# Scaling both halves of the inner RMS norms on VectorE, and issuing the local heads' O products one scheduling step later

## The chip, the cores and the metric

The kernel runs on one core of a Trainium2 chip. The metric is the device time of one execution in microseconds, as the median of several runs. TensorE is called PE here (its weight loads PEld), VectorE DVE, ScalarE ACT, GpSimd POOL and SyncE SP. Each engine executes its own instructions in the order in which the program lists them, and waits on semaphores for the others. A DMA is issued from the queue of one engine (here SP or POOL), in that queue's order.

## The reference

A two-layer decoder trunk on x of 512 tokens by 1024 features, in float32. Layer 0 mixes tokens by three groups of dilated window attention with 8 heads each, layer 1 by a gated linear recurrence. Each mixer and each ConvFFN stands between two RMS norms.

```python
for layer in range(DEPTH):                      # DEPTH = 2
    h = rms_norm(x, norm_mix_pre[layer])
    h = dilated_attention_mixer(h, ...) if layer % 2 == 0 else rglru_mixer(h, ...)
    x = x + rms_norm(h, norm_mix_post[layer])
    h = rms_norm(x, norm_ffn_pre[layer])
    h = conv_ffn(h, ...)
    x = x + rms_norm(h, norm_ffn_post[layer])
# rms_norm(x, g) = x * rsqrt(mean(x*x, -1) + 1e-6) * g
# attention, per head and group: o = softmax(q k^T * scale + bias, masked) v
# local group: window 128, dilation 1; its o is later mixed with the two strided groups by their softmax sums
```

## The kernel before

**Tiles.** The 512 tokens are four token tiles of 128 rows (t = 0 to 3). The normalised activations stand transposed in `hT` (feature on the partition, token along the row), as a rounded high part and a remainder (`hi`, `lo`). Each fp32 product is three PE passes: high times high, high times low, low times high. Weights are loaded as `raw` by DMA (some, called `sum`, are added up in memory by POOL's DMAs), split by ACT into `whi` (L253) and by DVE into `wlo` (L265), and kept in eight slots ahead of PE.

**Order.** The program is written out by hand: a stretch of PE products is followed by `tick()`, which lets side generators go on. A side that says `yield n` goes on n ticks later. So the numbers after `yield` place the side's instructions in every engine's order; nothing is reordered at run time.

**Local heads.** `local(h, ...)` is such a side, one for each of the 8 heads. It computes the scores `S` on PE (L1307), the biased row maxima on DVE (L1268) and the exponentials on ACT (L1323), transposes blocks on DVE (L1328), writes them to memory (`ltd`, L1283) and reads them back in the transposed place (`PT`, L1292), both from SP's queue. Then it says `yield 2`, and then multiplies `PT` with the values on PE into the bank `O` (L1346, 14 matmuls), copies it out on ACT (L1348) and writes it to memory from SP (`o0d`, L1350). Heads 0 and 1 wait after that `yield` for the values to exist, so that their place is set by the values.

**Inner norms.** There are three places where one sub-layer ends and the next one starts with a norm: attention to the first FFN (near 470 to 502 us of the span), first FFN to the recurrence (832 to 875 us) and recurrence to the second FFN (994 to 1024 us). At each, `norms` runs once for each token tile: `postnorm` reads the PE banks `acc`, squares them on ACT (L443, `junk`), multiplies by the gain on DVE (L547, `post`) and adds to x (L552). `prenorm` then squares x on ACT (L443), multiplies x by the gain on DVE (L477), gets the root on ACT (L450) and refines the reciprocal root on DVE with four small operations (L451 to L454), which leave two factors `y` and `q`, each one number for a row. L480 multiplies them to one factor; then the first half of the row (512 elements, `xs[0]`) is scaled on DVE (L481) and the second half (`xs[1]`) on ACT (L482). Three or four ticks later PE transposes both halves (L490, `tr`), ACT rounds them into `hT` (L499), and DVE takes the remainder (L500).

Of the kernel before, what the change touches and what calls it, by code (L numbers as in the profile page):

```python
# [14 lines left out]
AF = mybir.ActivationFunctionType  # L15
ALU = mybir.AluOpType
# [79 lines left out]
def kernel(  # L96
# [28 lines left out]
    nc = tc.nc  # L125
# [16 lines left out]
    def gen(dt=F32, s="g"):  # L142
        return gp.tile([P, 512], dt, tag="g", name=nm(s))

    def psum(s="ps"):
        return pp.tile([P, 512], F32, tag="ps", name=nm(s))

    def small(cols, s="s"):
        return sp.tile([P, cols], F32, tag=f"s{cols}", name=nm(s))
# [288 lines left out]
    def rms(parts, before=None, after=None):  # L438

        ss, b, v, y, q = small(2), small(1), small(1), small(1), small(1)  # L440
        for i, h in enumerate(parts):
            junk = gen(s="junk")
            nc.scalar.activation(junk, h, AF.Square, accum_out=ss[:, i : i + 1])  # L443
            if i == 0:
                if before:
                    before()
                nc.vector.tensor_scalar(b, ss[:, 0:1], 1.0 / D, EPS, op0=ALU.mult, op1=ALU.add)
        if after:
            after()
        nc.scalar.activation(y, ss[:, 1:2], AF.Sqrt, scale=1.0 / D, bias=b)  # L450
        nc.vector.scalar_tensor_tensor(v, ss[:, 1:2], 1.0 / D, b, op0=ALU.mult, op1=ALU.add)  # L451
        nc.vector.reciprocal(y, y)
        nc.vector.scalar_tensor_tensor(q, y, v, y, op0=ALU.mult, op1=ALU.mult)
        nc.vector.tensor_scalar(q, q, -0.5, 1.5, op0=ALU.mult, op1=ALU.add)  # L454
        return y, q
# [10 lines left out]
    def halves(ap):  # L466
        return [ap[:, 0:512], ap[:, 512:1024]]
# [4 lines left out]
    def prenorm(t, hT, g, wait, paired=True):  # L472
        xh, gh = halves(xs_sb[t]), halves(g)
        xs = [gen(s="xs") for _ in range(2)]

        def gained(i):
            nc.vector.tensor_tensor(xs[i], xh[i], gh[i], op=ALU.mult)  # L477

        y, q = rms(xh, lambda: gained(0), lambda: gained(1))
        nc.vector.tensor_tensor(q, y, q, op=ALU.mult)  # L480
        nc.vector.tensor_scalar(xs[0], xs[0], q, None, op0=ALU.mult)  # L481
        nc.scalar.activation(xs[1], xs[1], AF.Identity, scale=q)  # L482
        yield wait
        transposed(t, xs, hT, (0, 1), paired)

    def transposed(t, xs, hT, parts=(0, 1), paired=False):
        for i in parts:
            ps = psum("tr")
            for k in range(4):
                nc.tensor.transpose(ps[:, k * P : (k + 1) * P], xs[i][:, k * P : (k + 1) * P], ident)  # L490
            ps3 = ps.rearrange("p (k c) -> p k c", k=4)
            hi, lo = (h[:, 4 * i : 4 * i + 4, t * P : (t + 1) * P] for h in hT)
            if paired:
                ps3 = ps.rearrange("p (k c a) -> p k a c", k=4, a=2)
                hi, lo = (
                    h[:, 4 * i : 4 * i + 4, :].rearrange("p k (a c) -> p k a c", a=2)[:, :, :, 64 * t : 64 * t + 64]
                    for h in hT
                )
            nc.scalar.activation(hi, ps3, AF.Copy)  # L499
            nc.vector.tensor_tensor(lo, ps3, hi.bitcast(F32), op=ALU.subtract)  # L500
# [578 lines left out]
    def attention(hT, post, pre, spill):  # L1079
# [46 lines left out]
        def toeplitz(*which):  # L1126

            ask()
            key, T = asked.pop(0)
            assert key == which  # L1130
            return T
# [132 lines left out]
        def vtile(vs, t, part):  # L1264
            return vs[t].rearrange("p (b a) -> p a b", a=2)[:, part // 2, part % 2 * P : part % 2 * P + P]

        def scores(dst, ps, bias, mx, over=3 * NEG):
            nc.vector.tensor_tensor_reduce(  # L1268
                dst, ps, bias, scale=1.0, scalar=over, op0=ALU.add, op1=ALU.max, accum_out=mx
            )  # L1270

        def strips(t):
            return t.rearrange("p (j m k) -> p j m k", j=4, m=4)

        def in_strips(ap):
            return ap.rearrange("p (j k) -> p j k", j=4)

        def by_fours(ap):
            return ap.rearrange("p (k j) -> p j k", j=4)

        def to_dram(t, ms, name):
            d = dp.tile([P, 512], F32, name=name)
            nc.sync.dma_start(strips(d)[:, :, ms, :], strips(t)[:, :, ms, :])  # L1283
            return d

        def from_dram(d, ms):

            t = gen(s="PT")
            w = 32 * (ms.stop - ms.start)
            src = bass.AP(tensor=d.tensor, offset=d.offset + 32 * ms.start, ap=[[P, P], [32 * 512, 4], [1, w]])  # L1290
            dst = t.rearrange("p (i c) -> p i c", i=4)[:, :, 32 * ms.start : 32 * ms.stop]
            nc.sync.dma_start(dst, src)  # L1292
            return t.rearrange("p (i m q) -> p m i q", i=4, m=4)

        def weights_of(L, a, j0):
            m = 2 * (a % 2)
            return L[a // 2].rearrange("p (j c) -> p j c", j=4)[:, :, 32 * (m + j0) : 32 * (m + 2)]

        def local(h, hh, q, k, v):
            T = toeplitz(0, h)  # L1300
            L = [gen(s="L") for _ in range(2)]
            Sp = [psum("S") for _ in range(2)]
            mx = small(4)
            for a in range(4):
                o = (a % 2) * 256
                lo, k0 = (P, 0) if a == 0 else (0, (a - 1) * P)
                mm(Sp[a // 2][:, o + lo : o + 256], q[hh][:, a * P : (a + 1) * P], k[hh][:, k0 : (a + 1) * P],  # L1307
                   start=True, stop=True)
            for a in range(4):
                o = (a % 2) * 256  # L1310
                lo = P if a == 0 else 0
                for j in range(lo // P, 2):
                    c = slice(o + j * P, o + j * P + P)
                    scores(
                        strips(L[a // 2])[:, :, 2 * (a % 2) + j, :], in_strips(Sp[a // 2][:, c]), by_fours(T[:, j * P : j * P + P]),
                        mx[:, a : a + 1], mx[:, a : a + 1] if j and a else 3 * NEG,
                    )
            neg = small(4)
            nc.vector.tensor_scalar(neg, mx, -1.0, None, op0=ALU.mult)
            nc.vector.tensor_copy(st0[:, :, 0, h], mx)  # L1320
            for a in range(4):
                ls = weights_of(L, a, 1 if a == 0 else 0)
                nc.scalar.activation(ls, ls, AF.Exp, bias=neg[:, a : a + 1], accum_out=st0[:, a, 1, h : h + 1])  # L1323
            yield 1
            turned = [gen(s="LT") for _ in range(2)]
            skip = slice(1, 4), slice(0, 4)
            for c in range(2):
                nc.vector.transpose(strips(turned[c])[:, :, skip[c], :], strips(L[c])[:, :, skip[c], :])  # L1328
            yield 1
            placed = [to_dram(turned[c], skip[c], f"ltd{h}{c}") for c in range(2)]  # L1330
            yield 2
            pts = {}
            for c in range(2):
                pt = from_dram(placed[c], skip[c])
                for m in range(4):
                    pts[2 * c + m // 2, m % 2] = pt[:, m]
            yield 2
            if len(v) < 4:
                while len(v) < 4:
                    yield 1  # L1340
                yield 1 + h
            po = psum("O")
            for a in range(4):
                js = [1] if a == 0 else [0, 1]
                for j in js:
                    mm(po[:, a * P : (a + 1) * P], vtile(v, a - 1 + j, h % 4), pts[a, j], start=j == js[0], stop=j == 1)  # L1346
            o = gen(s="o0")
            nc.scalar.activation(o, po, AF.Copy)  # L1348
            od = dp.tile([P, 512], F32, name=f"o0d{h}")
            nc.sync.dma_start(od, o)  # L1350
            o0[h] = od
# [163 lines left out]
        for hp in range(4):  # L1515
            q, k = [], []
# [345 lines left out]
```

## Time and profile before

| what | value |
|---|---|
| median of 3 runs | 1384.68 us (1384.51 to 1389.64) |
| the profiled execution | 1389.3 us, its span 1387.5 us |
| PE busy | 1355.5 us (98%) |
| DVE busy | 1048.3 us (76%) |
| ACT busy | 679.5 us (49%) |
| POOL busy | 111.3 us (8%) |
| mean granted PE clock | 0.996 |
| moved by DMA | 243.11 MB |

The span runs from the first to the last instruction of the profiled execution; all starts are counted from its beginning. In a row of the timeline the columns are start, duration, engine, line, operation, output<-input and count, and in brackets the time for which the engine had been idle and what released it. In a row of the windows the clock (PEclk) stands behind the busy times of the five engines, then the DMA share. In a row of the waits stand total, count and longest wait.

### The profile page before, as it was taken

The page shows a single profiled execution, that of the slowest core. Times are in us where ns is not written, and L with a number is a line of the kernel's source. Part 1 is how long each engine was busy: PE and PEld are TensorE (multiplying, and loading weights), DVE is VectorE, ACT ScalarE, POOL GpSimd, SP SyncE. Part 2 cuts the span into 40 slices and gives each one's busy share as a digit, 9 for nine tenths or more (in the row PEclk, how much of TensorE's full clock was granted, in tenths as well). Part 3 has the DMA queues.
Part 4 walks back from the last instruction along what each step waited for, and adds up shares of the span by engine and source line. Part 5 has one row for each costly group of instructions (what it writes and reads, how often), then busy time and mean ns, then how long its engine had stood idle before and what let it go on. Part 6 is the DMA issues. An engine that isn't in the chain of part 4 may idle for free.

```text
span 1387.5 us, 18700 instructions
## 1 busy us (share of the span) xinstructions
PE 1355.5 (98%) x7109; PEld 1200.3 (87%) x7109; DVE 1048.3 (76%) x1838; ACT 679.5 (49%) x1137; POOL 111.3 (8%) x126
## 2 busy tenths in 40 slices
PE   8999999999999989999999999999999999999997
PEld 6888888888888889998888888888899998888886
DVE  7786574636767678897978789778878897958785
ACT  5434342414355563455545545579663455535452
POOL 1211012011000001000000020000001000000020
PEclk9999999999999999999999999999999999999999
DMA  8979679696648264565767793233153665758771
GB/s 256 241 219 276 161 181 262 199 217 180 222 154 305 85 187 103 158 167 127 193 183 193 200 269 126 92 122 121 61 156 99 167 167 128 187 161 213 206 203 61
DMA packets 184237, 243.11 MB, mean 175 GB/s; under 512 B 16632, under 2 KB 135936, under 8 KB 184146
## 3 DMA queue, kind: packets, MB, share of 16 engines
q1 hardware_dynamic: 151456, 184.82, 40.7%
q0 software_dynamic: 32688, 57.09, 21.4%
q8 instruction: 56, 0.92, 0.3%
q14 instruction: 35, 0.29, 0.1%
q10 hardware_dynamic: 2, 0.00, 0.0%
HBM read 218.23 MB, written 28.36 MB: 178 GB/s over the span
## 4 chain that ended last, share of the span: by engine, by line
PE 30%; DVE 25%; ACT 9%; DMA 4%; issue 3%; DVEq 0%; ACTq 0%; SPq 0%; POOLq 0%
PE ps L436 16%; DVE wlo L265 7%; PE vq L634 5%; PE acc L436 5%; DVE u L822 5%; PE vq L436 3%; ACT whi L253 2%; DMA sum<-in_ffn_w_down_dram 2%; DVE xb L1581 1%; DVE x L552 1%; ACT u L818 1%; DVE run L609 1%; DVE post L547 1%; DMA raw<-in_ffn_w_up_dram 1%; DVE u L834 1%
## 5 line engine op out<-in xcount | busy, mean ns | idle before, releaser
L436 PE MATMUL ps<-hT,whi 128*128 128x512 f32 (+1 forms) x2528 | 698.8, 362 | 2.1 <-DVE hT L500 1.5
L436 PEld LDWEIGHTS ps<-hT,whi 128*128 128x128 f32 x2528 | 460.1, 190 | 59.2 <-DVE hT L500 2.2
L436 PE MATMUL ps<-hT,wlo 128*128 128x512 f32 (+1 forms) x1264 | 456.6, 361 | 1.5 <-DVE wlo L265 1.5
L265 DVE TENSOR_TENSOR wlo<-raw,whi 128x1024 fp32r<-128x1024 f32 x233 | 280.0, 1217 | 24.5 <-ACT whi L253 24.2
L253 ACT ACTIVATE whi<-raw 128x1024 fp32r<-128x1024 f32 x233 | 239.0, 1051 | 119.8 <-DMA raw<-in_attn_w_qkv_dram 82.9
L436 PEld LDWEIGHTS ps<-hT,wlo 128*128 128x128 f32 x1264 | 240.3, 190 | 29.8 <-DVE wlo L265 1.9
L822 DVE SCALAR_TENSOR_TENSOR u<-ps,cols,u 128x511 f32<-128x511 f32 (+1 forms) x160 | 119.5, 747 | 71.2 <-ACT u L818 68.3
L253 ACT ACTIVATE whi<-sum 128x1024 fp32r<-128x1024 f32 x68 | 70.7, 1050 | 143.8 <-DMA sum<-in_ffn_w_down_dram 65.2
L634 PE MATMUL vq<-whi,A 128*128 128x512 f32 x448 | 137.8, 379 | 0.0
L265 DVE TENSOR_TENSOR wlo<-sum,whi 128x1024 fp32r<-128x1024 f32 x68 | 81.9, 1217 | 57.6 <-ACT whi L253 57.6
L436 PE MATMUL acc<-whi,alo 128*128 128x512 f32 x256 | 97.2, 380 | 1.7 <-DVE alo L185 1.6
L436 PE MATMUL acc<-whi,ahi 128*128 128x512 f32 x256 | 98.2, 383 | 0.0
L436 PE MATMUL acc<-wlo,ahi 128*128 128x512 f32 x256 | 97.2, 380 | 0.6 <-DVE wlo L265 0.6
L634 PEld LDWEIGHTS vq<-whi,A 128*128 128x128 f32 x448 | 84.7, 189 | 12.0
L634 PE MATMUL vq<-wlo,A 128*128 128x512 f32 x224 | 85.1, 380 | 2.1 <-DVE wlo L265 2.1
L832 ACT ACTIVATE u<-u 128x512 f32<-128x512 f32 x48 | 30.3, 632 | 110.4 <-DVE u L822 110.4
L818 ACT ACTIVATE u<-ps,cols 128x512 f32<-128x512 f32 x80 | 61.0, 763 | 4.6 <-PE ps L436 4.6
L634 PE MATMUL vq<-whi,T 128*128 128x512 f32 x192 | 59.7, 382 | 0.0
L436 PEld LDWEIGHTS acc<-whi,alo 128*128 128x128 f32 x256 | 48.4, 189 | 9.2 <-DVE alo L185 2.5
L436 PEld LDWEIGHTS acc<-wlo,ahi 128*128 128x128 f32 x256 | 48.4, 189 | 7.8 <-DVE wlo L265 1.4
L436 PEld LDWEIGHTS acc<-whi,ahi 128*128 128x128 f32 x256 | 48.4, 189 | 6.6 <-ACT ahi L184 0.2
L634 PEld LDWEIGHTS vq<-wlo,A 128*128 128x128 f32 x224 | 42.3, 189 | 8.8 <-DVE wlo L265 2.9
(247 smaller groups left out, 1782.3 us busy)
## 6 DMA issues: line engine op xcount, KB each, us to landing
raw<-in_ffn_w_up_dram SPq DMA_DIRECT2D x44, 1024.0 KB
raw<-in_attn_w_qkv_dram SPq DMA_DIRECT2D x25, 1024.0 KB
raw<-in_ffn_w_down_dram SPq DMA_DIRECT2D x16, 1024.0 KB
sum<-in_ffn_w_down_dram POOLq DMA_DIRECT2D x16, 1024.0 KB, 8.7
sum<-in_attn_w_qkv_dram POOLq DMA_DIRECT2D x24, 512.0 KB, 8.4
raw<-in_attn_w_qkv_dram SPq DMA_DIRECT2D x16, 512.0 KB
sum<-in_ffn_w_down_dram SPq DMA_DIRECT2D x8, 1024.0 KB
raw<-in_lru_w_in_dram SPq DMA_DIRECT2D x8, 1024.0 KB
```

Of the source, the lines that this page charges most:

```text
L253: nc.scalar.activation(hi, raw, AF.Copy)
L265: nc.vector.tensor_tensor(lo, raw, hi.bitcast(F32), op=ALU.subtract)
L436: mm(dst, l[a], r[b], start=start and n == 0, stop=stop and n == 2)
L547: nc.vector.tensor_tensor(in_two(u[i]), unwoven(banks[i]), in_two(gh[i]), op=ALU.mult)
L552: nc.vector.scalar_tensor_tensor(xh[i], u[i], y, xh[i], op0=ALU.mult, op1=ALU.add)
L609: nc.vector.tensor_tensor(r[h], a, b[:, k], op=ALU.add if sg > 0 else ALU.subtract)
L634: mm(banks[u], act(a)[:, 2 * j + k, u * P : (u + 1) * P], woven(W[b][:, k, :]), start=(j, k, n) == (0, 0, 0), stop=(j, k, n) == (1, 1, 2),)
L818: nc.scalar.activation(u, ps, AF.Identity, scale=cc[:, j : j + 1], bias=cc[:, 48 + j : 49 + j])
L822: nc.vector.scalar_tensor_tensor(u[:, d:], ps[:, : S - d], wc, u[:, d:], op0=ALU.mult, op1=ALU.add)
L832: nc.scalar.activation(u, u, AF.Gelu_apprx_tanh)
L834: nc.vector.tensor_tensor(gv[k], gv[k], u, op=ALU.mult)
L1581: nc.vector.scalar_tensor_tensor(u[:, d:], ps[:, : S - d], wc, u[:, d:], op0=ALU.mult, op1=ALU.add)
```

## The change

```diff
         y, q = rms(xh, lambda: gained(0), lambda: gained(1))
-        nc.vector.tensor_tensor(q, y, q, op=ALU.mult)
-        nc.vector.tensor_scalar(xs[0], xs[0], q, None, op0=ALU.mult)
-        nc.scalar.activation(xs[1], xs[1], AF.Identity, scale=q)
+        for i in range(2):
+            nc.vector.tensor_scalar(xs[i], xs[i], y, q, op0=ALU.mult, op1=ALU.mult)
         yield wait
         transposed(t, xs, hT, (0, 1), paired)
...
                 pt = from_dram(placed[c], skip[c])
                 for m in range(4):
                     pts[2 * c + m // 2, m % 2] = pt[:, m]
-            yield 2
+            yield 3
             if len(v) < 4:
```

The first edit is executed 12 times (three places, four token tiles). DVE loses the product of two columns (L480) and gains the second half; both halves are now multiplied by two factors in one operation. ACT loses L482. All other instructions keep their order. Lines after L480 are one lower in the changed kernel.

The second edit moves the O product of heads 2 to 7, each with its ACT copy and its SP write; heads 0 and 1 keep their place. POOL's order is unchanged.

On PE, before, in the third pair of local heads. `O_1289` is head 0, `O_1301<-PT_1204` is head 2, and `S_1317` are the scores of head 4:

```order
L1346 MATMUL O_1289<-PT_924,c_363 128x128 x2
L1346 MATMUL O_1289<-PT_924,c_364 128x128
L1346 MATMUL O_1301<-PT_1204,v_365 128x128 x2
L1346 MATMUL O_1301<-PT_1204,v_366 128x128
L1346 MATMUL O_1301<-PT_1206,v_366 128x128
L1346 MATMUL O_1301<-PT_1206,c_363 128x128 x2
L1346 MATMUL O_1301<-PT_1206,c_364 128x128
L1307 MATMUL S_1317<-qk_1165,qk_1000 128x128
L1307 MATMUL S_1317<-qk_1165,qk_1000 128x256
```

Head 2's product stands directly behind head 0's, and head 4's scores behind it. The same place on PE now:

```order
L1345 MATMUL O_1289<-PT_924,c_363 128x128 x2
L1345 MATMUL O_1289<-PT_924,c_364 128x128
L1306 MATMUL S_1305<-qk_1165,qk_1000 128x128
L1306 MATMUL S_1305<-qk_1165,qk_1000 128x256
L1306 MATMUL S_1306<-qk_1165,qk_1000 128x256 x2
L436 MATMUL ps_1330<-hT_85,whi_1129 128x512
```

The scores follow head 0 at once, then a feature product of 24 matmuls into `ps_1330`. Behind that product PE now has head 1 and then head 2 (`PT_1204`):

```order
L1345 MATMUL O_1357<-PT_962,c_363 128x128 x2
L1345 MATMUL O_1357<-PT_962,c_364 128x128
L1345 MATMUL O_1369<-PT_1204,v_365 128x128 x2
L1345 MATMUL O_1369<-PT_1204,v_366 128x128
L1345 MATMUL O_1369<-PT_1206,v_366 128x128
L1345 MATMUL O_1369<-PT_1206,c_363 128x128 x2
L1345 MATMUL O_1369<-PT_1206,c_364 128x128
L1306 MATMUL S_1389<-qk_1201,qk_1056 128x128
```

So head 2 is one feature product later. Head 3 likewise goes behind two value products of 24 matmuls each.

On DVE, before, at the end of token tile 3's norm in the first place (`s_4482` is `y`, `s_4483` is `q`, `tr_4552` belongs to token tile 2, `tr_4590` to tile 3):

```order
L453 SCALAR_TENSOR_TENSOR s_4483<-s_4482,s_4481 128x1
L454 TENSOR_SCALAR s_4483<-s_4483 128x1
L480 TENSOR_TENSOR s_4483<-s_4482,s_4483 128x1
L481 TENSOR_SCALAR xs_4477<-xs_4477,s_4483 128x512
L500 TENSOR_TENSOR hT_3933<-tr_4552,hT_3932 128x8x64
L500 TENSOR_TENSOR hT_3933<-tr_4559,hT_3932 128x8x64
L500 TENSOR_TENSOR hT_3933<-tr_4590,hT_3932 128x8x64
```

And now:

```order
L453 SCALAR_TENSOR_TENSOR s_4480<-s_4479,s_4478 128x1
L454 TENSOR_SCALAR s_4480<-s_4480 128x1
L481 TENSOR_SCALAR xs_4474<-xs_4474,s_4479,s_4480 128x512
L481 TENSOR_SCALAR xs_4475<-xs_4475,s_4479,s_4480 128x512
L499 TENSOR_TENSOR hT_3933<-tr_4548,hT_3932 128x8x64
L499 TENSOR_TENSOR hT_3933<-tr_4555,hT_3932 128x8x64
L499 TENSOR_TENSOR hT_3933<-tr_4586,hT_3932 128x8x64
```

The small product is gone and the second half stands behind the first, ahead of tile 2's remainders. On ACT, before, at the same place:

```order
L450 ACTIVATE s_4482<-s_4479,s_4480 128x1
L482 ACTIVATE xs_4478<-xs_4478,s_4483 128x512
L499 ACTIVATE hT_3932<-tr_4552 128x8x64
L499 ACTIVATE hT_3932<-tr_4559 128x8x64
L499 ACTIVATE hT_3932<-tr_4590 128x8x64
```

And now:

```order
L450 ACTIVATE s_4479<-s_4476,s_4477 128x1
L498 ACTIVATE hT_3932<-tr_4548 128x8x64
L498 ACTIVATE hT_3932<-tr_4555 128x8x64
L498 ACTIVATE hT_3932<-tr_4586 128x8x64
L498 ACTIVATE hT_3932<-tr_4593 128x8x64
```

Between the root (L450) and token tile 2's evictions ACT no longer has anything that waits for DVE's factors. In the same way, after L450 of tiles 0 and 2 in the first place the next on ACT is now the squaring of the next tile's banks, and after L450 of tile 1 the next weight split (`whi`).

## Prediction

> **What bounds the kernel now.** I read the page's head first, then the waits of PE, then the timeline of PE at the longest of them, and last the timeline of DVE and ACT ahead of those.
>
> ```profile
> span 1387.5 us, 18700 instructions
> PE 1355.5 (98%) x7109; PEld 1200.3 (87%) x7109; DVE 1048.3 (76%) x1838; ACT 679.5 (49%) x1137; POOL 111.3 (8%) x126
> ...
> PE tr L490 <- DVE xs L481: 7.1, 5, 3.1
> PE O L1346 <- DMA PT<-ltd: 2.2, 1, 2.2
> ...
> PE ps L436 <- DVE wlo L265: 1.5, 1, 1.5
> ```
>
> PE is the bound: 98% busy, the rest a few waits. An edit can gain only in what PE waits for, and in PE's clock. The two longest entries are what this change touches: the transposes of the inner norms wait 7.1 us for the scaled rows, and one O product waits 2.2 us for `PT` from memory.
>
> **The O products.** PE's timeline at the third pair of heads, and the same work a little later without a wait:
>
> ```profile
> 133.29 1.68 PE L1346 MATMUL O<-PT,v 128*128 128x128 f32 x8 [2.17 <-DMA PT<-ltd]
> ...
> 136.04 2.44 PE L1307 MATMUL S<-qk,qk 128*128 128x128 f32 x8
> 138.13 0.78 PE L436 MATMUL ps<-hT,whi 128*128 128x512 f32 x2
> ...
> 143.50 1.10 PE L1346 MATMUL O<-PT,v 128*128 128x128 f32 x8
> ...
> 145.14 1.11 PE L1346 MATMUL O<-PT,v 128*128 128x128 f32 x8
> ...
> 146.79 1.68 PE L1307 MATMUL S<-qk,qk 128*128 128x128 f32 x8
> 148.12 0.57 PE L634 MATMUL vq<-whi,hT 128*128 128x512 f32 x1
> ```
>
> The head-2 product starts 2.17 us late, and is then slow itself: 136.04 - 133.29 = 2.75 us against 146.79 - 145.14 = 1.65 us for the same 14 matmuls; the scores behind it take 138.13 - 136.04 = 2.09 against 148.12 - 146.79 = 1.33 us. That is 1.1 + 0.8 = 1.9 us more. The windows say why:
>
> ```profile
> 133.30:136.00 2.70, 2.70 (x14) 2.60 (x15) 0.00 (x0) 0.00 (x0) 0.00 (x0) 0.66 1.10 341
> ...
> 501.00:503.00 2.00, 1.95 (x18) 1.95 (x19) 1.25 (x3) 2.00 (x5) 0.00 (x0) 1.00 0.90 296
> ...
> 872.50:875.00 2.50, 2.50 (x14) 2.50 (x13) 0.73 (x1) 0.42 (x1) 0.00 (x0) 0.53 0.13 52
> ```
>
> The granted clock was 0.66 behind this wait. It was also 0.53 at 872.5 to 875 us, behind a row of smaller waits in the second norm place, which cost there (1 - 0.53) x 2.5 = 1.2 us; and it stayed at 1.00 at 501 us, behind the longest wait of all (3.15 us, below). So a dip follows some waits and not others.
>
> The edit puts 1.33 us of scores and a product of 24 matmuls (5.4 us, as from 138.13 to 143.50) ahead of head 2, and head 1's product (1.65): PE reaches it near 133.29 - 2.17 + 1.33 + 5.37 + 1.65 = 139.5 us, and `PT` was there at 133.3. The wait goes whole: 2.2 us, and the 1.9 us with it. What else is moved: for heads 2 to 7, 14 matmuls with their weight loads, an ACT copy and an SP write each. PE does the same work in another order, at no cost. On ACT the copy of head 3 now waits for a product behind two value products; behind it stand weight splits that PE uses a product and more later (10 us), which is their cover; without it PE would wait about 1 us for each. On SP the write of head 3 goes behind a weight load and two value writes, so that this load no longer queues behind it; POOL's order is the same, and its table loads wait for score maxima, which come earlier with PE. The `PT` buffers are held one step longer; two later `PT` loads now wait for PE, for products over some 10 us before. Next to be late after this is the weight remainder at 359 us (1.5 us, above).
>
> The Trainium skill ("TensorE: Matmul & The Clock Gate", Part 1) says that the clock is halved after an idle window of about 3.4 us on a free-running grid. The dip here came behind 2.17 us, so the trace does not bear out that length, and by that rule the dip would not be this wait's; the sum without it is the third rival.
>
> **The norms.** First the price of a scale with two factors, which the trace does not have.
>
> ```profile
> L552 DVE SCALAR_TENSOR_TENSOR x<-post,s,x 128x512 f32<-128x512 f32 x32 | 22.6, 748 | 0.6
> L481 DVE TENSOR_SCALAR xs<-xs,s 128x512 f32<-128x512 f32 x12 | 5.8, 486 | 0.4
> L1629 DVE TENSOR_SCALAR th<-th 128x512 f32<-128x512 f32 x8 | 3.4, 426 | 0.3
> ...
> L453 DVE SCALAR_TENSOR_TENSOR s<-s,s 128x1 f32<-128x1 f32 x28 | 6.1, 219 | 1.0
> L451 DVE SCALAR_TENSOR_TENSOR s<-s,s 128x1 f32<-128x1 f32 x28 | 4.2, 150 | 0.0
> ```
>
> A column as a factor costs 60 to 69 ns over a constant (486 against 426, 219 against 150). So two factors: 486 + 60 = 546 ns, my value, as the nearest form; the low end is 486 (the second factor costs nothing), the high end 748 (the rate of the operation with two tensors).
>
> The Trainium skill ("VectorE: DVE Perf Modes", the perf-mode tier table) lets a float32 scale from SBUF run at two elements a cycle, and names no charge for factors. By it the operation stays at 486 ns and the sum below is 1.1 us lower.
>
> ```profile
> 472.07 0.16 DVE L480 TENSOR_TENSOR s<-s,s 128x1 f32<-128x1 f32 x1
> 473.59 0.69 DVE L547 TENSOR_TENSOR post<-acc,gain 128x512 f32<-128x512 f32 x1 [0.84 <-ACT junk L443]
> 479.05 0.16 DVE L480 TENSOR_TENSOR s<-s,s 128x1 f32<-128x1 f32 x1
> 480.95 1.23 DVE L265 TENSOR_TENSOR wlo<-raw,whi 128x1024 fp32r<-128x1024 f32 x1 [1.21 <-ACT whi L253]
> 493.33 0.16 DVE L480 TENSOR_TENSOR s<-s,s 128x1 f32<-128x1 f32 x1
> 494.85 0.69 DVE L547 TENSOR_TENSOR post<-acc,gain 128x512 f32<-128x512 f32 x1 [0.84 <-ACT junk L443]
> ...
> 836.59 0.16 DVE L480 TENSOR_TENSOR s<-s,s 128x1 f32<-128x1 f32 x1
> 838.49 2.36 DVE L265 TENSOR_TENSOR wlo<-raw,whi 128x1024 fp32r<-128x1024 f32 x2 [1.22 <-ACT whi L253]
> 847.74 0.16 DVE L480 TENSOR_TENSOR s<-s,s 128x1 f32<-128x1 f32 x1
> 849.17 1.29 DVE L500 TENSOR_TENSOR hT<-tr,hT 128x512 fp32r<-128x512 f32 x2 [0.75 <-ACT hT L499]
> 860.82 0.16 DVE L480 TENSOR_TENSOR s<-s,s 128x1 f32<-128x1 f32 x1
> 861.42 0.68 DVE L648 TENSOR_TENSOR c<-acc,c 128x512 f32<-128x512 f32 x1
> 868.17 0.16 DVE L480 TENSOR_TENSOR s<-s,s 128x1 f32<-128x1 f32 x1
> ...
> 1015.83 0.69 DVE L547 TENSOR_TENSOR post<-acc,gain 128x512 f32<-128x512 f32 x1 [0.84 <-ACT junk L443]
> ...
> 478.00 0.30 ACT L450 ACTIVATE s<-s,s 128x1 f32<-128x1 f32 x1
> ...
> L253 ACT ACTIVATE whi<-raw 128x1024 fp32r<-128x1024 f32 x233 | 239.0, 1051 | 119.8 <-DMA raw<-in_attn_w_qkv_dram 82.9
> ```
>
> Where nothing waits (860.82 to 861.42), L480 and L481 occupy DVE for 0.60 us, of which 0.20 is L480; so one scale takes a slot of 0.40, with two factors 0.46, and the new pair 0.92 us. Alone that is 0.32 us more on DVE per tile. But in most tiles DVE does not go on after 0.60 us: it waits 0.75 to 1.22 us for ACT, which has to finish its own scale (L482) before it squares the next tile's banks, splits a weight or evicts a transpose. With L482 gone, ACT starts these right after L450: for tile 1 of the first place the split is ready by 478.00 + 0.30 + 1.05 (a split on ACT) = 479.35, and DVE takes over when its pair is done. The pair thus fits into the wait. By chain, first place:
>
> - tile 0: 472.07 + 0.92 = 472.99 instead of 473.59: 0.60 earlier;
> - tile 1: 479.05 - 0.60 + 0.92 = 479.37 instead of 480.95: 1.58 earlier;
> - tile 2: 493.33 - 1.58 + 0.92 = 492.67 instead of 494.85: 2.18 earlier;
> - tile 3: its first half is ready 0.20 + 0.49 - 0.55 = 0.14 sooner after L480 than now. In all 2.3 us.
>
> ```profile
> 501.05 1.09 PE L490 MATMUL tr<-ident,xs 128*128 128x128 f32 x8 [3.15 <-DVE xs L481]
> ...
> 868.91 1.09 PE L490 MATMUL tr<-ident,xs 128*128 128x128 f32 x8 [0.84 <-DVE xs L481]
> ...
> 871.55 0.58 PE L436 MATMUL ps<-hT,whi 128*128 128x256 f32 x1 [0.57 <-DVE hT L500]
> ...
> 1022.15 1.09 PE L490 MATMUL tr<-ident,xs 128*128 128x128 f32 x8 [0.84 <-DVE xs L481]
> ```
>
> The 2.3 us come off the wait of 3.15 at 501.05 and the shorter ones ahead of it in the same place, since PE reaches the transposes earlier too. Second place: 836.59 + 0.92 against 838.49 is 0.98 earlier, 847.74 - 0.98 + 0.92 against 849.17 is 1.49; at 861.42 DVE waits for nobody and 0.32 are lost, 1.17 left. Tile 3's L480 is then at 867.00, its pair done at 867.92, and tile 2's two remainders (1.29 together, as at 849.17), which no longer wait for ACT, at 869.2; tile 3's first one ends at 869.9, and PE, which now starts behind it at 871.55, gains 1.7 us. Third place: ahead of tile 3 stands the same wait of 0.84 (1015.83), so again 0.60, and 0.14, off the 0.84 at 1022.15: 0.7 us. Norms together 2.3 + 1.7 + 0.7 = 4.7 us. With 486 ns it is 5.8, with 748 ns (a pair of 1.34 us) by the same chain 0.9 + 0 + 0.1 = 1.0 us. PE's second half of the transposes is covered: it needs `xs[1]` 0.4 us after the first, and DVE delivers it 0.46 after.
>
> **The sum.** Against the profiled execution: 1389.3 - 4.7 - 2.2 - 1.9 = 1380.5 us, and 1379.3 if the dip at 872.5 us goes with the waits ahead of it. But this execution lies 4.6 us above the median of 1384.68, beside the slowest run (1389.64). The trace cannot tell what the other two runs lack; the sizes fit two answers. Without the two dips (3.1 us of it) they have 4.7 + 2.2 left to gain: 1377.8. Without head 2's wait and its dip (4.1 us) they have 4.7 left: 1380.0. I take 1379.0 us, 0.4% below the median. A difference under 0.5% is about what a measurement of this kernel can't tell from none.
>
> **The rivals.**
>
> 1. The O gain is only moved. Weights come through latencies of DMA and ACT, and PE, 2 to 4 us earlier, waits for the remainder at 359 us instead. For it speaks that this wait is there now (1.5 us); against it that the loads are issued when PE frees a slot, and so come earlier too. Price: 2.2 to 4.1 us back, about 1382.5. Chance 0.15.
> 2. The scale with two factors runs at the rate of 748 ns: norms 1.0 instead of 4.7, so 1382.7. Against it: a second factor needs no second tensor. Chance 0.08.
> 3. The slow clock at 133 us belongs to the load at that time and stays, with the wait gone: 1380.9. Within my own range.
> 4. More than forecast: all the PE waits at the second norm place go, and the dip with them in every run: about 1375.5. Chance 0.12.
> 5. Slower: DVE becomes the bound in the norm places, if the two-factor form is slower than any float32 row of this width, at 1.2 us. The pair then takes 2.3 us, more than the 1.4 to 1.9 us it has in tiles 0 and 1, and by the chain the three places lose 2.5 + 3.9 + 1.3 = 7.7 instead of gaining 4.7: about 1391.4. Norms begin to lose from about 0.8 us. Against it: 486 ns with one factor. Chance 0.05.
>
> The forecast (1376.5 to 1381.5) has 0.60. Half a per cent below the median is 1377.8: rival 4 and about two fifths of the forecast lie under it, 0.12 + 0.24 = 0.36. Slower by as much (above 1391.6) is about rival 5, 0.05; the rest, 0.59, is the same. The range of 1375.0 to 1383.5 leaves out rival 5, about half of rival 4 and the ends of the others.
>
> **What would show it.** In the profile after: no wait of O for `PT`, and a clock of 1.00 from 131 to 139 us; L481 24 times at about 546 ns and no L482; DVE's waits of 0.84 for `junk` and of 1.2 for `whi` gone in the norm places; the waits of the first place together some 2.3 us shorter; no transpose wait in the third place. I am wrong if L481 is above 0.8 us, if PE's wait for `wlo` near 359 us has grown by what the O products gave, or if a PE wait for a bank held by ACT shows up behind the O products.

## The result, and the profile after

| kernel | median, us | runs | against the kernel before in the same session |
|---|---|---|---|
| before | 1384.6 | 6 | |
| changed | 1376.49 | 6 (1373.78 to 1379.52) | 0.9932 [0.9906, 0.9959] |
| changed, timed again on another occasion | 1376.57 | 7 | 0.9944 [0.9924, 0.9965] |

The changed kernel is faster by 0.6 to 0.7%, 7 to 8 us. The forecast was 1379.0. The ratios here and below are taken over fast runs alone, which leaves out one run of 2924 us of the kernel before and one of 1568 us further down, and they need not be the quotient of two medians. The changed kernel's profiled execution took 1376.62 us (span 1374.9), that of before 1389.3, so these two traces differ by 12.7 us, more than the medians do.

First the group of the new scale in the changed kernel (busy us, mean ns of one, DVE's idle time before it), then PE's waits (us in total, times, longest):

```profile
L481 DVE TENSOR_SCALAR xs<-xs,s,s 128x512 f32<-128x512 f32 x24 | 12.2, 550 | 0.4
```

```profile
PE tr L489 <- DVE xs L481: 4.0, 3, 2.6
PE vq L633 <- DVE wlo L265: 2.0, 2, 1.2
...
PE ps L436 <- DVE hT L499: 0.6, 1, 0.6
...
PE ps L436 <- DVE wlo L265: 0.2, 1, 0.2
```

The scale with two factors takes 550 ns in the mean. The waits for `xs` went from 7.1 to 4.0 us, the wait of O for `PT` is gone, that for the remainder near 359 us fell from 1.5 to 0.2. New in this place of the table are 2.0 us of the value products in the first FFN. The rows themselves, from PE's timeline (the last column is PE's idle time before the row, and what ended it):

```profile
139.04 1.11 PE L1345 MATMUL O<-PT,v 128*128 128x128 f32 x8
...
485.48 1.08 PE L489 MATMUL tr<-ident,xs 128*128 128x128 f32 x8 [0.70 <-DVE xs L481]
491.84 1.49 PE L489 MATMUL tr<-ident,xs 128*128 128x128 f32 x8 [2.60 <-DVE xs L481]
...
707.44 0.48 PE L633 MATMUL vq<-wlo,A 128*128 128x512 f32 x1 [1.16 <-DVE wlo L265]
...
711.11 0.48 PE L633 MATMUL vq<-wlo,A 128*128 128x512 f32 x1 [0.81 <-DVE wlo L265]
...
862.68 1.23 PE L489 MATMUL tr<-ident,xs 128*128 128x128 f32 x8 [0.72 <-DVE xs L481]
865.04 0.38 PE L436 MATMUL ps<-hT,whi 128*128 128x256 f32 x1 [0.64 <-DVE hT L499]
```

And DVE in the first place:

```profile
465.10 1.00 DVE L481 TENSOR_SCALAR xs<-xs,s,s 128x512 f32<-128x512 f32 x2
466.02 0.68 DVE L546 TENSOR_TENSOR post<-acc,gain 128x512 f32<-128x512 f32 x1
...
471.48 1.00 DVE L481 TENSOR_SCALAR xs<-xs,s,s 128x512 f32<-128x512 f32 x2
472.40 3.49 DVE L265 TENSOR_TENSOR wlo<-raw,whi 128x1024 fp32r<-128x1024 f32 x3
```

The pair starts at 465.10 and DVE goes on at 466.02 without a wait for `junk`, at 472.40 without one for `whi`: a slot of 0.92 us, and the ACT waits behind it are gone. The starts of the same PE work in both traces show where the lead comes from:

| PE work | before | after | lead |
|---|---|---|---|
| first feature product (L436) behind the later O products | 158.67 | 154.13 | 4.5 |
| scores that waited for `qk` (0.74) before | 413.98 | 407.00 | 7.0 |
| first product behind tile 3's transposes, first place | 501.90 | 492.98 | 8.9 |
| value products of the first FFN | 541.28 | 533.70 | 7.6 |
| features of the first FFN behind the new wait | 718.66 | 713.59 | 5.1 |
| tile 2's transposes, second place | 861.65 | 855.57 | 6.1 |
| gate products behind the second place | 894.18 | 886.11 | 8.1 |
| tile 3's transposes, third place | 1022.15 | 1013.01 | 9.1 |
| features late in the second FFN | 1242.37 | 1230.64 | 11.7 |

Two steps of this table are no part of the change's own places: 1.3 us less waiting near 355 us, and 2.06 us of waits at 1236 and 1240 us that the changed kernel's trace lacks. Two steps go back: 8.9 to 7.6 and 7.6 to 5.1. The second is mostly the new wait of 2.0 us. The first is the clock (columns from the left: the stretch, its length, busy time of PE, PEld, DVE, ACT and POOL with counts, the granted clock, DMA share, GB/s):

```profile
131.00:139.00 8.00, 8.00 (x45) 7.21 (x45) 4.76 (x18) 2.99 (x8) 0.58 (x1) 1.00 1.13 330
488.99:492.40 3.41, 0.81 (x8) 0.61 (x7) 3.30 (x11) 2.30 (x7) 0.00 (x0) 1.00 0.57 186
492.40:495.81 3.41, 3.41 (x18) 3.41 (x18) 3.11 (x5) 3.04 (x5) 0.80 (x1) 0.50 0.82 278
```

The dip at head 2 is gone; one of the same kind now stands behind the wait of 2.60 us.

### The profile page after: what moved, and what is told of

Same layout as the page of the kernel before. It is cut to its first block, busy times and chain, and to the rows that moved or that the text cites. A ratio compares the mean times of both kernels' runs of the same rounds, so it can differ in the third digit from the quotient of the medians.

```text
span 1374.9 us, 18692 instructions
## 1 busy us (share of the span) xinstructions
PE 1354.0 (98%) x7109; PEld 1199.2 (87%) x7109; DVE 1052.6 (77%) x1838; ACT 671.5 (49%) x1125; POOL 111.3 (8%) x126
## 4 chain that ended last, share of the span: by engine, by line
PE 46%; DVE 32%; ACT 11%; DMA 7%; issue 3%; DVEq 0%; SPq 0%; ACTq 0%; POOLq 0%
PE ps L436 24%; PE vq L633 10%; DVE wlo L265 9%; DVE u L821 8%; PE acc L436 7%; DMA sum<-in_ffn_w_down_dram 3%; ACT whi L253 3%; ACT u L817 2%; DVE run L608 2%; DMA raw<-in_ffn_w_down_dram 1%; DVE u L833 1%; ACT u L831 1%; DVE xb L1580 1%; PE O L1465 1%; PE S L1386 1%
## 5 line engine op out<-in xcount | busy, mean ns | idle before, releaser
L436 PE MATMUL ps<-hT,whi 128*128 128x512 f32 (+1 forms) x2528 | 698.4, 362 | 0.8 <-DVE hT L499 0.6
L436 PEld LDWEIGHTS ps<-hT,whi 128*128 128x128 f32 x2528 | 459.9, 190 | 57.5 <-ACT whi L253 1.3
L436 PE MATMUL ps<-hT,wlo 128*128 128x512 f32 (+1 forms) x1264 | 456.4, 361 | 0.2 <-DVE wlo L265 0.2
L436 PEld LDWEIGHTS ps<-hT,wlo 128*128 128x128 f32 x1264 | 240.1, 190 | 28.5 <-DVE wlo L265 0.6
L436 PE MATMUL acc<-whi,alo 128*128 128x512 f32 x256 | 97.3, 380 | 1.2 <-DVE alo L185 1.2
L436 PE MATMUL acc<-whi,ahi 128*128 128x512 f32 x256 | 98.2, 383 | 0.0
L436 PE MATMUL acc<-wlo,ahi 128*128 128x512 f32 x256 | 97.1, 379 | 0.2 <-DVE wlo L265 0.2
L436 PEld LDWEIGHTS acc<-whi,alo 128*128 128x128 f32 x256 | 48.4, 189 | 9.1 <-DVE alo L185 2.4
L436 PEld LDWEIGHTS acc<-wlo,ahi 128*128 128x128 f32 x256 | 48.4, 189 | 7.1 <-DVE wlo L265 0.6
L436 PEld LDWEIGHTS acc<-whi,ahi 128*128 128x128 f32 x256 | 48.4, 189 | 6.6 <-ACT ahi L184 0.2
```

The source lines that it names most:

```text
L436: mm(dst, l[a], r[b], start=start and n == 0, stop=stop and n == 2)
```

## The experiments

**The two edits apart, and the norm edit taken to pieces.** These four were timed together.

The norm edit alone (the diff of `prenorm`; `yield 2` stays):

> The norm edit alone; the O products stay at the old step. Theory A (the two edits add up, each by what PE waits for): the time is the kernel before's less the norm part. By the changed kernel's trace, whose lead over before grows from 6.0 us ahead of the first norm place to 8.9 behind it and from 5.1 to 9.1 over the second and third, with a new slow stretch of 1.7 us in the first place, the norm part is 4.5 to 6 us: about 0.9960 of before, 1379 us against 1384.6. The head-2 product still waits 2.2 us for PT near 131 us, and DVE's waits of 0.84 for junk are gone as in the changed kernel. Theory B (the lead is mostly the O edit's and the execution's, the norms give back what they gain in the slow clock): over 0.9980, 1382 us or more.

Measured: 1380.1 us, 0.9969 [0.9952, 0.9986]: 4.3 us by the ratio, 2.8 by the medians, and between the two theories' figures. PE's waits for `xs` are those of the changed kernel, which speaks for theory A. The head-2 wait was not 2.2 us:

```profile
131.93 0.50 PE L1346 MATMUL O<-PT,v 128*128 128x128 f32 x2 [0.20 <-DMA PT<-ltd]
...
493.73 1.60 PE L490 MATMUL tr<-ident,xs 128*128 128x128 f32 x8 [2.60 <-DVE xs L481]
```

The O edit alone (`yield 3`; `prenorm` as before):

> The O edit alone; the norms keep L480 and the ACT scale. Theory A: the lead at 160 us is 4.1 to 4.5 us over the profiled execution of before and reaches the end, less the dip where the other executions lack it: 2.2 to 4.5 us, about 0.9975 of before (1381 us against 1384.6). PE waits about 7 us for xs in the norm places, in the same places as before (0.84 in the third). Rival 1 of the prediction (the lead turns into a longer wait for wlo near 355 us): no gain, 0.9995, and that wait is over 3 us. Theory C (most of the changed kernel's gain is this edit's): 0.995 or less.

Measured: 1379.97 us, 0.9977 [0.9959, 0.9996]. Its waits:

```profile
PE tr L490 <- DVE xs L481: 7.0, 5, 3.1
PE ps L436 <- DVE wlo L265: 1.9, 1, 1.9
```

No wait of O for `PT`. The wait for `wlo` near 355 us is 1.9 us here, not the 3 of the first rival. The shares gained by the two edits, 0.31 and 0.23%, make 0.54%, and the two timings of both together gave 0.68 and 0.56%: within the intervals they add up.

L480 kept, both halves on DVE with one factor:

```
-        for i in range(2):
-            nc.vector.tensor_scalar(xs[i], xs[i], y, q, op0=ALU.mult, op1=ALU.mult)
+        nc.vector.tensor_tensor(q, y, q, op=ALU.mult)
+        nc.vector.tensor_scalar(xs[0], xs[0], q, None, op0=ALU.mult)
+        nc.vector.tensor_scalar(xs[1], xs[1], q, None, op0=ALU.mult)
```

> The changed kernel, but with L480 kept: both halves scaled by DVE with the one factor q. If the gain of the norms comes from ACT being free of its scale (my theory), this stays near the changed kernel: DVE has 0.20 + 0.40 + 0.40 = 1.00 us a tile where the two-factor pair takes 0.92, so 0.08 us in each of the tiles whose chain PE waits for, at most 0.5 us in all: ratio to before within 0.001 of the changed kernel's 0.9932, PE's waits for xs 4 to 4.5 us. If it came from the dropped L480 (0.2 us a tile, and the first half earlier), the waits for xs are near 6 us and half the norm gain is lost: 0.995 to 0.996.

Measured: 1376.69 us, 0.9958 [0.9945, 0.9972]. By the ratio this is not what my theory gave (within 0.001 of 0.9932); it lies in the rival's 0.995 to 0.996. But the changed kernel itself came to 0.9944 when it was timed again, so the ratio can't tell the two apart. The waits can: they are 4.6 us, 0.6 longer than in the changed kernel and not the rival's 6:

```profile
PE tr L490 <- DVE xs L481: 4.6, 3, 2.7
```

DVE's waits of 0.84 for `junk` and 1.21 for `whi` in the first place are gone here too. And the kernel with the O edit alone differs from this one only in the engine that scales the second half: its median was 1379.97 in the same session, 3.3 us more.

The second half on ACT again, with L480 behind the first half:

```
-        for i in range(2):
-            nc.vector.tensor_scalar(xs[i], xs[i], y, q, op0=ALU.mult, op1=ALU.mult)
+        nc.vector.tensor_scalar(xs[0], xs[0], y, q, op0=ALU.mult, op1=ALU.mult)
+        nc.vector.tensor_tensor(q, y, q, op=ALU.mult)
+        nc.scalar.activation(xs[1], xs[1], AF.Identity, scale=q)
```

> The changed kernel, but the second half scaled by ACT again: DVE scales the first half with two factors, then multiplies y by q (L480, now behind it), then ACT scales the second half. The first half is 0.14 us earlier than before, the second 0.46 later, and ACT is as busy as before. If the norm gain is ACT's release, it is gone or turned round: DVE waits 0.84 and more for junk and 1.2 and more for whi in the norm places as before, PE waits 7 us or more for xs, and the time is that of the O edit alone or 1 to 3 us longer, 0.9975 to 0.9995. If the gain is the missing L480 ahead of the first half, the time is the changed kernel's, 0.993.

Measured: 1387.49 us, 1.0027 [1.0013, 1.0042], slower than the kernel before although the O edit is in it, and beyond the 0.9975 to 0.9995 that I gave. PE's waits, and two rows of DVE:

```profile
PE tr L490 <- DVE xs L480: 8.3, 4, 3.3
...
PE tr L490 <- ACT xs L482: 1.2, 5, 0.3
```

```profile
469.67 0.69 DVE L547 TENSOR_TENSOR post<-acc,gain 128x512 f32<-128x512 f32 x1 [1.36 <-ACT junk L443]
477.60 3.49 DVE L265 TENSOR_TENSOR wlo<-raw,whi 128x1024 fp32r<-128x1024 f32 x3 [1.74 <-ACT whi L253]
```

DVE's waits for ACT, 0.84 and 1.21 before, are 1.36 and 1.74: both longer by 0.5 us, by which ACT gets its scale later. Together the two runs show what the norm gain is: ACT freed of its scale. With that and L480 kept, most of the gain stays; with L480 out of the first half's way and ACT still scaling, it is lost and more. Against the O edit alone this kernel is 7.5 us slower: 2.5 us are longer waits for `xs` (9.5 against 7.0), 2.3 us are slow clock (a mean granted clock of 0.9948 against 0.9965, twelve runs each), and the rest is not traced.

**The kernel before once more**, for a second profiled execution.

> The kernel before once more, for a second profiled execution of it. The prediction took the first one's 1389.3 us as 4.6 us above what the kernel usually takes, and so took off either the wait and slow clock at head 2 (4.1 us) or the two slow stretches (3.1 us). If that was right, this execution shows no wait for PT near 131 us, or a clock of 1.00 from 131 to 139 and at 872 us. If the waits belong to the kernel and only the slow stretches move about, it waits again for PT (0.2 to 2.2 us) and 7.0 us for xs, and is slow in those stretches of 3.41 us, on a grid of that length, that come behind a stretch in which PE idled for 1.7 us or more: with a wait of 3.15 us in the first norm place, nine times in ten somewhere between 494 and 503 us.

It took 1379.06 us (one run), 3.8 us below this kernel's median in the same session, so that it is a draw from the other side and not the usual execution:

```profile
131.08 0.97 PE L1346 MATMUL O<-PT,v 128*128 128x128 f32 x6 [0.61 <-DMA PT<-ltd]
132.44 0.50 PE L1346 MATMUL O<-PT,v 128*128 128x128 f32 x2 [0.38 <-DMA PT<-ltd]
...
495.33 1.97 PE L490 MATMUL tr<-ident,xs 128*128 128x128 f32 x8 [3.16 <-DVE xs L481]
```

```profile
491.79:495.20 3.41, 0.38 (x4) 0.19 (x2) 3.27 (x11) 2.09 (x6) 0.00 (x0) 1.00 0.42 158
495.20:498.61 3.41, 3.28 (x16) 3.28 (x17) 2.61 (x5) 3.15 (x6) 0.00 (x0) 0.50 0.94 300
```

The norm waits are the same to 0.1 us. The wait for `PT` is 1.0 us and not 2.17; no dip follows it. The clock is 1.00 from 131 to 139 and at 872 us, which was the sign of the second reading. But two dips are not what this execution lacks: one stands in the first norm place instead, between 494 and 503 us as the rival said, behind the same 3.15 us that had none in the first execution. In all it is 10.2 us shorter than the first one. PE idles for 23.1 us instead of 32.0, and of these 8.9 us 1.2 are the wait for `PT`, none the norm places, and 7.7 waits that neither edit touches: above all two for `wlo` at 1236 and 1240 us (2.06), one for the remainder at 359 (1.50) and one for `alo` at 1351 (1.65). So the distance of an execution from the median says little of the change's own places.

**The price of DVE's time**: each half scaled once more.

```
             nc.vector.tensor_scalar(xs[i], xs[i], y, q, op0=ALU.mult, op1=ALU.mult)
+            nc.vector.tensor_scalar(xs[i], xs[i], 1.0, None, op0=ALU.mult)
```

> The changed kernel with each half scaled once more by DVE, by the constant 1.0 (24 operations of some 0.43 us): the pair of a tile then takes about 1.6 us of DVE instead of 0.92. By the prediction's chain (0.92: 4.7 us gained, 1.34: 1.0 gained, 2.3: 7.7 lost, so about 8.8 us for each us of the pair) that costs 0.7 x 8.8 = 6 us: near 1383 us, 0.999 of before, with PE waiting about 10 us for xs in the norm places and 1 to 2 us in the third, where the changed kernel waits for none. The rival, that DVE has slack and only ACT's release counts: within 1 us of the changed kernel (0.9935 to 0.996), waits for xs near 4 us.

Measured: 1390.65 us, 1.0062 [1.0038, 1.0086]: 14 us over the changed kernel, not 6.

```profile
PE tr L490 <- DVE xs L482: 10.9, 11, 3.1
PE vq L634 <- DVE wlo L265: 4.9, 3, 2.9
```

The pair came to 1.84 us of DVE (473.11 to 474.95 us at tile 1), not 1.6, for which the chain gives 0.92 x 8.8 = 8 us. The waits for `xs` are 10.9 us, 6.9 more than in the changed kernel. What the chain leaves out is the rest: 2.9 us more in the FFNs, and three dips of 1.7 us where the changed kernel's trace has one, 3.4 us. 6.9 + 2.9 + 3.4 = 13.2 us, of the 16.5 by which the two traces differ. The rival, that DVE has slack, is out.

**Which heads matter**: `yield 3 if h == 2 else 2`.

> The changed kernel, but only head 2's O product is one step later; those of heads 3 to 7 stand where they stood before. If the one wait for PT at head 2 is the whole of what the O edit gives (my theory), this is the changed kernel's time (0.9932 to 0.996 of before), with no wait of O for PT and the same lead at 200 us. If heads 3 to 7 have part in it, by waits that show only in some executions, a wait of O for PT or a late DVE operation stands behind head 3, and it is 1 to 3 us longer.

Measured: 1378.67 us without the run of 1568 us, 0.9970 [0.9954, 0.9985]. No wait of O for `PT`, and a lead of 4.2 to 4.5 us over the first trace of before at 176 us, as with all heads moved (4.5 us at 154). The time is 2.1 us over the changed kernel's second timing, which was taken on another occasion. That is the rival's price, and 0.9970 lies outside the range of my theory; but the rival's sign, a wait of O behind head 3, is not in the profile, and the intervals of the ratios overlap. Whether heads 3 to 7 have a small part in it stays open.

**One step more**: `yield 4`.

> The changed kernel with yield 4 in place of yield 3: the O products of heads 2 to 7 one more step later. PT was there at 131 to 133 us in five profiles, and PE reaches head 2 at 139 in the changed kernel, so one more step has nothing left to gain: the run above within 0.001, no wait of O for PT, the lead over before at 200 us 4 to 5 us. If head 2's margin were short in executions that no profile shows, it would be 1 to 2 us better; if the later products hold up the PT buffers or the score steps, 1 us or more worse.

Measured: 1376.53 us, 0.9949 [0.9930, 0.9968]: the same. One more step brings nothing that can be measured.

**Filler on PE against the slow clock.** In `transposed`, where `warm` is 6 for tile 3 of the first norm place and 0 everywhere else:

```
             ps = psum("tr")
+            for n in range(warm if i == 0 else 0):
+                mm(ps[:, 0:P], ident, ident, start=True, stop=True)
```

> The changed kernel with six products of the identity with itself on PE ahead of tile 3's transposes in the first norm place, written to the bank that the transposes overwrite: PE has about 1.6 us of work in its wait of 2.60 us. Five profiles of this kernel and its variants have slow stretches of 3.41 us, each costing 1.71 us, that begin on multiples of 3.413 us from one another within an execution, and each follows a stretch of the same grid in which PE idled for 1.8 us or more (once 1.4); stretches with 1.65 us and less of idling were followed by none otherwise. By that, a wait cut to 1.0 us can't be followed by a slow stretch at any phase: the clock is 1.00 from 485 to 505 us, and the time is 1.71 us x 0.7 (the share of phases at which 2.60 us put 1.75 into one stretch) = 1.2 us below the changed kernel. If what counts is the wait for data itself, or the products come late because the bank is not free, the clock still falls to 0.5 behind it, and the time is the same or up to 1.6 us longer.

Measured: 1374.38 us, 0.9949 [0.9929, 0.9968]. Then again, beside the changed kernel:

> The changed kernel once more, timed beside the two below. If the parts add up (0.9969 for the norm edit and 0.9977 for the O edit, each against the kernel before), this is 0.9946 of before; its first time was 0.9932, with an interval that holds both. In the profile the waits of the norm places are as in its first one (xs: 4.0 us in three waits); which of the first place's waits a slow stretch follows, and whether the value products wait for wlo in the first FFN, may differ.

> The changed kernel with the six filler products once more, beside the changed kernel itself. If the filler's worth is the slow stretch that it prevents, 1.71 us in some seven of ten executions, it is 1.2 us (0.001) below the run above; its first time, 1374.4 us, lay 2.1 below the changed kernel's first, but they were not timed together. If it is worth nothing, the two agree within 0.5 us. No slow stretch between 485 and 505 us.

Measured: changed kernel 1376.57, 0.9944 [0.9924, 0.9965]; with filler 1373.75, 0.9933 [0.9913, 0.9953]. Timed together, the median with filler is 2.8 us below that of the changed kernel, and the mean 1.9. The intervals of the ratios overlap, and the first timing's 0.9949 is no better than the changed kernel's two ratios, so that it beats the changed kernel is likely and not certain. From the first filler run's PE timeline, and the second's windows:

```profile
488.52 1.50 PE L489 MATMUL tr<-ident 128*128 128x128 f32 x12
491.20 1.17 PE L491 MATMUL tr<-ident,xs 128*128 128x128 f32 x8 [1.18 <-DVE xs L481]
```

```profile
485.00:505.00 20.00, 18.83 (x169) 18.50 (x167) 14.93 (x31) 11.20 (x18) 1.32 (x1) 1.00 0.58 159
```

The clock is 1.00 over the whole place, where the changed kernel's two profiles fell to 0.50 for 3.41 us. But over all timed executions the clock hardly differs: a mean of 0.9978 in 13 runs of the changed kernel and of 0.9980 in the 12 runs with filler at tile 3, which is 0.2 us of time, give or take 0.4, where I expected 1.2. The likelier source of the gain is another wait: that of the value products near 707 us (2.0 us in both profiles of the changed kernel) is gone too in both profiles with filler. Why was asked with the last run, the filler at tile 2:

> The changed kernel with the six filler products one tile earlier, ahead of tile 2's transposes in the first norm place, where PE waits 0.69 us and not 2.60. Open is why the value products of the first FFN wait 2.0 to 2.8 us for wlo near 707 us in all seven profiles that have the norm edit without filler, and in neither of the two with it. If twelve more instructions on PE are what matters (where its code loads fall against the weight sums), that wait is gone here too, and the time is about 2 us below the changed kernel's, 0.993 of before, less 0.8 us of filler that the 0.69 us wait doesn't cover. If it matters that PE comes to the first FFN without the wait of 2.60 us, the wait for wlo is here as in the changed kernel (2.0 us or more), and the time is the changed kernel's, 0.9944, within 1 us. In the first norm place PE then waits 1.8 us for tile 3, and a slow stretch may or may not follow.

Measured: 1373.63 us, 0.9930 [0.9904, 0.9956]. That wait is gone here as well, and PE waits at tile 3 nearly as long as without filler:

```profile
490.88 1.08 PE L491 MATMUL tr<-ident,xs 128*128 128x128 f32 x8 [2.16 <-DVE xs L481]
```

So it is not the missing wait at tile 3 that spares the first FFN its wait. All seven profiles in which DVE scales both halves and PE has no filler show 2.0 to 2.8 us of it; of the seven others (before twice, the O edit alone, the ACT scale, and the three with filler) none has it in the first FFN, though the first execution of before has the same 2.06 us in the second. Twelve matmuls more on PE take it away at either tile.

The traces show where the 2 us come from. The value products wait for a weight that SP loads and POOL's DMA then adds to (`sum`). From SP's issue of the load to the landing of POOL's DMA it takes 20.1 to 20.3 us in the seven profiles with the wait, and 16.0 to 16.2 us in the seven without. In the changed kernel SP issues at 682.75 and ACT starts to split the sum at 702.96 us; with filler at tile 2 it is 679.85 and 695.98. The two groups differ in one more thing: a 16 KB packet of the DMA queue for instructions (q8) starts 1.0 to 3.5 us behind SP's issue in all seven with the wait, and in the others 0.1 to 0.4 or 4.4 to 4.8 us behind it. That fits twelve more matmuls shifting such loads. It is not shown as the cause: behind the next load of the same kind, with filler at tile 2, a packet at 2.7 us goes with no delay.

## Why the prediction was right, and where it was off

The time fell within the range, 2.5 us below the forecast value, at the very edge of the 1376.5 to 1381.5 to which I had given 0.60, and below the 1377.8 us that marked half a per cent, to which I had given 0.36. It lies near the fourth rival's 1375.5 with half of its mechanism: in the second norm place no dip stands in the changed kernel's two profiles, but 1.36 us of waits remain.

- **Price of the scale.** 546 ns was taken, 550 in the mean and 545 in the median measured; the pair's slot is the 0.92 us of the sum. The Trainium skill ("VectorE: DVE Perf Modes", the perf-mode tier table) names no charge for a factor; the trace has one of some 60 ns over the 486 of one factor.
- **Norms, 2.3 + 1.7 + 0.7 us.** The waits of the first place were 0.93 + 1.22 + 3.15 = 5.3 us and are 0.70 + 2.60 = 3.3: 2.0. Second place: 1.04 + 0.84 + 0.60 + 0.57 = 3.05, now 0.72 + 0.64 = 1.36: 1.7. Third: 0.84, now none: 0.8. In all 4.5 against 4.7; alone, the edit measured 4.3 us (0.31% of 1382.9; 1.9 to 6.6). The mechanism, ACT released a scale earlier, is shown by the pair of kernels that keep L480 or keep ACT. Not foreseen were the 2.0 us that this edit brings at 707 us; that the sum of the norms came out so well alone is partly luck, since a gain in the clock (below) made up for them.
- **O products, 2.2 + 1.9 us.** The wait goes whole, and PE reaches head 2 at 139.04 where 139.5 was said. But both sizes belong to one execution. The wait is 2.17 there, 1.0 and 0.2 in the others that have the old place; and the mean granted clock is 0.9965 in the twelve runs of the O edit alone and 0.9967 in the 35 of before beside them, so that the 1.9 us of slow clock are no part of its gain in the mean. Alone the edit measured 3.2 us (0.6 to 5.7), more than the three waits' mean of 1.1; whether there is more to it stays open. The first rival, the wait for the remainder near 355 us, came out as neither a loss nor a gain of the edit: that wait is 1.50, 0 and 0.2 us in the three profiles with the old place, and 0 to 1.9, in the mean 0.6, in the eleven with the new one.
- **The step that failed** is the last of the sum. I took the 4.6 us by which the first execution lay above the median as waits or dips of the change's own places that the other executions lack, and subtracted them from the gain: 1379.0 instead of 1384.68 - 4.7 - 2.2 - 1.9 = 1375.9. The second execution of before has the norm waits to the full, and a dip as well, in another place; what sets the two apart is mostly waits that neither edit touches (7.7 of 10.2 us). That 1375.9 would have been so near is in part luck too, since the O edit has no 1.9 us of clock in the mean.
- **The clock's part of the gain.** The dips move about: five in the three profiles with the old norm code (before twice, O edit alone), five in the six with the new one and no added work (two with the norm edit alone, one in each of the changed kernel's two and with head 2 alone, none with L480 kept or with `yield 4`). The granted clock of every timed run says it better: in the mean 0.9964 in 74 runs of before and 0.9978 in 13 of the changed kernel. That is 5.0 and 3.0 us lost, of which the kernel's last stretch takes 1.3 to 2.9 in the profiles. So some 2 us, about one dip, are part of the gain. In the separate runs the norm edit has 1.1 us of it and the O edit none. I had no such term.
- **The slow clock.** I held that a dip after 2.17 us and none after 3.15 do not bear out a fixed window, and made a slow clock that stays without the wait the third rival. It was this wait's: without it the clock is 1.00 from 131 to 139 us, and with a wait of 1.0 us as well. Each dip cost 1.71 us; I had read 1.9 and 1.2, the second from a window that cut the dip short. How they lie is told in the last section.
- **DVE as the bound** (the fifth rival) is real: with a pair of 1.84 us the kernel is slower than before by 0.6%, where the chain and the O edit's 3.2 us would leave it about as fast as before.

## What to carry to other kernels

Where a wait on the critical chain ends with an engine that is busy with a share of the work it could give away, the price to weigh is the release of that engine, not the operation count: here 0.32 us more on DVE a tile took away DVE waits for ACT of 0.75 to 1.22 us. A single execution's waits on a DMA, and the slow stretches of the clock, move about between executions; ask for the expected size of each before a difference to the median is explained by one of them. Work for PE that needs nothing, put into a wait, kept the clock at 1.00 in the profiles; that it is worth time for this reason was not shown here. And since twelve more matmuls went with the loss of a wait 215 us later, the whole table of waits has to be read, not only the place that was edited.

## What the runs showed of the hardware

The slow stretches of PE's clock lie on a grid. In fourteen profiles sixteen of them stand ahead of the kernel's end, and each lasts 3.4 us at 0.50, a loss of 1.71 us (the edges from windows of 0.1 us). Within an execution their starts are whole multiples of 3.413 us apart: 134.2 and 871.4 in before (216 steps), 494.1 and 869.6 with the norm edit alone (110), and with the ACT scale 497.9, 863.1 and 1023.6 (107 and 47). Which stretch turns slow is read from PE's busy time in the one ahead. Before, first execution:

```profile
130.79:134.20 3.41, 1.24 (x10) 0.95 (x9) 0.00 (x0) 0.00 (x0) 0.00 (x0) 1.00 1.13 317
134.20:137.61 3.41, 3.41 (x14) 3.23 (x14) 0.04 (x1) 0.29 (x1) 0.00 (x0) 0.50 1.15 305
496.01:499.43 3.42, 1.89 (x17) 1.70 (x16) 3.28 (x11) 1.59 (x5) 0.00 (x0) 1.00 0.04 18
499.43:502.84 3.41, 1.79 (x16) 1.79 (x17) 2.52 (x9) 2.42 (x6) 0.00 (x0) 1.00 0.88 297
```

The wait of 3.15 us straddled an edge: 1.53 us of idling in one stretch and 1.62 in the next, and neither made the following one slow; the wait of 2.17 us lay in one stretch whole, and did. In fifteen of sixteen cases PE had idled 1.79 us or more in the stretch ahead; once 1.4 was enough (869.6 us, norm edit alone), and once 1.94 was not (the kernel with L480 kept, its grid taken from its end); up to 1.76 us none followed otherwise. Near the kernel's end one more escaped, with some 1.85 us (filler at tile 2). No run sets the idling alone, so this is a bound read from fourteen traces and no measured threshold. The Trainium skill ("TensorE: Matmul & The Clock Gate", Part 1) speaks of a free-running window of about 3.4 us, and the grid agrees. It asks for an idle window; here one that is idle for about half is enough.

Twelve more matmuls on PE in the first norm place went with the loss of a wait of 2.0 to 2.8 us some 215 us later, with or without the long wait in the norm place. The weight sum that this wait hangs on took 16.0 to 16.2 us from SP's issue to its landing in those executions, and 20.1 to 20.3 in those with the wait; why stays open.
